# Hybrid attention/SSD layer in float32: the product of probabilities and values, the spacing of three short chains, and what is kept of the scaled tokens

## The chip, the cores and the metric

The kernel runs on one NeuronCore of one Trainium2 chip. The metric is the device time of one execution in microseconds (us). Engines are named as the profile names them: PE (TensorE matmuls), PEld (its weight loads), DVE (VectorE), ACT (ScalarE), POOL (GpSimd), SP (SyncE, which here only issues DMAs).

## The reference

One decoder layer on 2048 tokens of width 1024, everything in float32, then a final norm. Cut to its steps:

```python
mod = silu(c) @ w_ada + b_ada                    # shift1, scale1, gate1, shift2, scale2, gate2
h = modulate(rmsnorm(x, norm1_w), shift1, scale1)
q, k, v, z, xbc, dt = split(h @ w_in)            # 8 query heads, 2 key/value heads of 64
attn = sliding_window_attention(rope(q), rope(k), v, sinks)   # window 128, blocks of 128
xs, B, C = split(silu(causal_depthwise_conv(xbc)))
y = ssd_chunked_scan(xs, softplus(dt), A, B, C, d_skip)       # chunks of 128
y = group_rmsnorm(y * silu(z)) * ssm_norm_w
x = x + gate1 * (concat(attn, y) @ w_out)
h = modulate(rmsnorm(x, norm2_w), shift2, scale2)
x = x + gate2 * ((silu(h @ w_g) * (h @ w_u)) @ w_down)        # width 2816
out = rmsnorm(x, final_norm_w)
```

In the attention, for each block of 128 queries, `probs` (128 queries by 256 keys for each head) is multiplied with `v` (256 keys by 64).

## The kernel before, in words

**Tiling.** The 2048 tokens are four blocks `b` of 512 (`T`), each of four chunks of 128 (`P`). Dense projections run as pieces: one output tile in a PSUM bank (four `d` banks; four side banks `am`, `at`, `sm`, `st` belong to the mixers). Precision is kept by splitting each operand into a rounded part `hi` (type fp32r, written by ACT) and a rest `lo` (a subtraction on DVE or POOL); `mm3` (lines 280 to 282) then issues three fp32r matmuls: hi by hi, hi by lo, lo by hi.

**Order of the work.** Until the gate/up projection of the feed-forward part, PE runs in the order of the program text (`manual_schedule` of PE). There a main stream of projection pieces (`queries`, `keys_values`, `convolved`, `gated`, `out_proj`) is cut by `yield`s; after each piece `tick` lets a side stream advance by one step. Side streams are the attention (`attentions`), the SSD scan (`ssds`), the norms of later blocks, and the operands of the next stage. DVE, ACT, POOL and SP are ordered by the scheduler's own simulation when the program is built; each runs its instructions in that order, so an instruction that waits holds up all behind it on its engine. From the gate/up quads on (`quad`, lines 978 to 980), PE too is ordered by the scheduler.

**Probabilities times values.** For each chunk and each half of the heads, `transposed` (line 671) turns two tiles of probabilities on PE into the banks `am` and `at`; ACT copies each to `hi` (line 677) and DVE subtracts to get `lo` (line 678). One step later `values` (line 680) multiplies with the values. `v_ring` holds hi and lo of the values of two chunks, each padded with 64 zero columns, so that every stationary tile is 128 keys by 128 columns with one of the two key/value heads in its half and zeros in the other; `mm3` is called for each of two chunks and two heads, all four adding into one bank of 128 by 256. These are 12 fp32r matmuls of 256 columns for a half, 6 in the first chunk of all. ACT then copies the result out (line 688). `load_values` fills `v_ring` by an ACT cast (626) and a POOL subtraction (627).

**Norms.** `rstd`/`root_of_sum` give one factor for each token; `spread` (line 321) builds diagonal tiles with four DVE operations (line 324) and multiplies them by ones on PE (line 326), so that the factors stand along the free axis in a bank.

**Short chains.** `convolved` ends each piece with a chain over ACT (496, 497), DVE (498, 499), POOL (500), ACT tanh (501), DVE (502) and a store. `ssds` ends each chunk with sums of squares on ACT, an inverse root by 13 small POOL operations (250 to 255), and a scaling on ACT (805); one chunk later `turned` (line 723) transposes the result on PE (726). `out_proj` (line 819) loads its residual `x` (833, 834) after the matmuls of a piece, adds (835), and stores it to `mid` (836).

**Operands of the gate/up stage.** During the last projections (`conv`, `gated(3)`), `operands_first`, `operands_between` and `sums_ahead` read tiles of `mid`, scale them by the norm's factors (DVE, line 883), and build the operands of seven block products; `sums_ahead` leaves its four sums in DRAM (`raw_d`), from where `operands_kept` reads them when the quads begin.

Of the kernel before, what the change touches and what calls it, by code (L numbers as in the profile page):

```python
# [18 lines left out]
P = 128  # L19
# [3 lines left out]
T = 512  # L23
# [21 lines left out]
def hymba_layer(ctx, tc, xT, xtok, pos, wada, wadk, vecs, rows, wq, wkv, wz, wx, wo, wgu, wd, outT):  # L45
# [27 lines left out]
    def tmp():  # L73
        return big("t", TMP, pool=fw)
# [111 lines left out]

    def behind(engine):
        traced = nc.cur_bb.bb.instructions
        return tc.issue_after(next(i for i in reversed(traced) if i.engine == engine))
# [131 lines left out]
    def spread(y, eng=nc.vector, bc=None):  # L321
        dg, n = tmp(), y.shape[1]
        for t in range(n):
            spread.last = eng.tensor_scalar(dg[:, t * P:(t + 1) * P], ident, y[:, t:t + 1], 0.0, ALU.mult, ALU.add)
        bc = (norm_bank() if bc is None else bc)[:, 0:n * P]
        nc.tensor.matmul(bc, ones, dg[:, 0:n * P], start=True, stop=True)
        return bc
# [23 lines left out]
    def norm1(b, h):  # L351
# [9 lines left out]
        y = root_of_sum(ms, NT)  # L361
        yield
        bc = big("bc", 1, pool=xp)
        nc.scalar.copy(bc, spread(y))
# [115 lines left out]
    def convolved(b, h):  # L480
        for c in range(8):
            ps = dense()
            for half in range(2):
                if half:
                    yield
# [15 lines left out]
            nc.scalar.activation(th, cv, AF.Tanh)  # L501
            nc.vector.scalar_tensor_tensor(o, th, 1.0, cv, ALU.add, ALU.mult)
            nc.sync.dma_start(xs_d[b][c], o)
# [16 lines left out]
    v_ring = const([P, 4 * 192 + 64], "v_ring", F32R)  # L520
    nc.gpsimd.memset(v_ring.bitcast(F32), 0.0)
# [39 lines left out]
    def attentions(b, m):  # L561
        late = []

        def values_of(sms, slots, t):
            got = {}

            def turn(half):
                pT = [m.m4().rearrange("p h t -> p (h t)").rearrange("p (b j k) -> p b j k", b=4, j=2)
                      for _ in range(2)]
# [52 lines left out]
    def load_values(kv, slot):  # L622
        v = kv[:, P:2 * P].rearrange("p (r d) -> p r d", d=64)
        vhi, vlo = (v_ring[:, at:at + 256].rearrange("p (r d) -> p r d", d=P)[:, :, 0:64]
                    for at in (slot * 192, (2 + slot) * 192))
        nc.scalar.copy(vhi, v)
        nc.gpsimd.tensor_tensor(vlo, v, vhi.bitcast(F32), ALU.subtract)
# [42 lines left out]
    def transposed(sm, pT, ns, at):  # L670
# [5 lines left out]
        hi, lo = (pT[i][:, 0:2 * ns, at, :] for i in range(2))  # L676
        nc.scalar.activation(hi, ps, AF.Copy)
        nc.vector.tensor_tensor(lo, ps, hi.bitcast(F32), ALU.subtract)

    def values(out, pT, slots, half):  # L680
        po = bank("am", 1)[:, 0:2 * P]
        for s, slot in enumerate(slots):
            for r in range(2):
                b = 2 * s + r
                vhi, vlo = (v_ring[:, at:at + P] for at in (slot * 192 + r * 64, (2 + slot) * 192 + r * 64))
                phi, plo = (pT[i][:, b].rearrange("p j q -> p (j q)") for i in range(2))
                mm3(po, vhi, vlo, phi, plo, b == 0, b == 2 * len(slots) - 1)
        nc.scalar.copy(out[:, half * 2 * P:(half + 1) * 2 * P], po)

    def ssds(b, stepping, m):  # L690
# [22 lines left out]
        def decays(u, cbt):  # L713
# [7 lines left out]
            return dm  # L721

# [9 lines left out]
        for t in range(NT):  # L732
# [24 lines left out]
            u = factors(t, 1)  # L757
            yield
            if out:
                turned(*out)  # L760
                yield
# [41 lines left out]
            for g in range(2):  # L803
                gs = slice(g * 256, (g + 1) * 256)
                nc.scalar.activation(y[:, gs], y[:, gs], AF.Copy, scale=rs[:, g:g + 1])
            out = (y, o, ts)
            yield
        yield
        turned(*out)
# [12 lines left out]
    def out_proj(b, y_of, mix, bank_of, acc, norm=None, each=lambda c: None):  # L822
        for c in range(KT):
            ps = bank_of(c)
            for half in range(2):
                if half:
                    yield
# [5 lines left out]
            x = tmp()  # L833
            nc.sync.dma_start(x, xT[b, c])
# [64 lines left out]
    def operands_first(s, ops, bc):  # L899
# [4 lines left out]
        for k in range(4):  # L904
# [4 lines left out]
            if s:  # L909
                for i in range(2):  # L910
                    nc.sync.dma_start(scaled_d[i][k], h[i, 0])
# [4 lines left out]
    scaled_d = [[dr.tile([P, T], F32, name=f"scaled{i}{k}") for k in range(4)] for i in range(2)]  # L916
# [803 lines left out]
```

## Time and profile before

| | us |
|---|---|
| three timed runs of the kernel before | 2227.67, 2231.42, 2234.55 (median 2231.42) |
| the profiled execution's own time | 2235.22 |
| its span, first to last instruction | 2233.2 |
| PE busy in the span | 2167.6 (97%) |
| DVE, ACT, POOL busy | 1692.5 (76%), 1011.3 (45%), 572.5 (26%) |
| mean granted TensorE clock | 0.988 of full speed |

How to read it: a row of the groups gives line, engine, operation, output from input, shapes, count, then busy time in us and the mean ns of one, then the idle time of the engine just before these instructions and what ended it. Matmuls overlap in the pipeline, so the mean of one is longer than the distance between the starts of two that follow each other; the distance is what counts in a full queue. A float32 matmul (not fp32r) shows as two PE instructions. Names are those of the program's tiles without buffer numbers (`m` is a working tile of the mixers, `t` a tile of the ring `tmp()` of eight).

### The profile page before, as it was taken

Reading aid. Unit: us, or ns where it says so; the run is one execution under the profiler, and the core shown is the slowest. Engines: PE = TensorE matmul, PEld = TensorE weight load, DVE = VectorE, ACT = ScalarE, POOL = GpSimd, SP = SyncE. Lnnn points to the kernel's source line nnn. Section 1 sums busy time; section 2 is a strip of 40 time slices with the busy share of each in tenths; the row PEclk is TensorE's granted clock in tenths of the full one; section 3 lists DMA queues with packets and bytes.
Section 4 is the critical chain, followed back from the end, with each engine's and each line's share of the span. In section 5 each row is a group of like instructions: output and inputs, shape, how many; then the busy total and the mean of one; then the engine's idle time right before and its main releaser. Section 6 shows DMA issues by size and latency. Waiting matters only on the chain.

```text
span 2233.2 us, 33604 instructions
## 1 busy us (share of the span) xinstructions
PE 2167.6 (97%) x11108; PEld 1808.3 (81%) x11108; DVE 1692.5 (76%) x3219; ACT 1011.3 (45%) x2137; POOL 572.5 (26%) x715
## 2 busy tenths in 40 slices
PE   8979999999999899999999999999999999999998
PEld 6879897879778778888888887788888888788887
DVE  6887757777669877788887768878878875786575
ACT  3674535544444655534434535533333333544452
POOL 0213434223102311145343122242332331110011
PEclk9999999999999999999999999999999999999999
DMA  7997789786989623234333678835555535778553
GB/s 272 329 344 274 253 258 345 261 289 206 318 299 303 192 94 104 86 117 128 105 103 129 222 261 270 295 120 169 188 163 190 173 105 204 261 265 265 183 171 102
DMA packets 289181, 469.93 MB, mean 210 GB/s; under 512 B 27376, under 2 KB 97008, under 8 KB 289008
## 3 DMA queue, kind: packets, MB, share of 16 engines
q1 hardware_dynamic: 288432, 467.27, 62.9%
q8 instruction: 87, 1.43, 0.3%
q14 instruction: 86, 0.70, 0.1%
q10 hardware_dynamic: 576, 0.52, 0.1%
HBM read 334.98 MB, written 132.71 MB: 209 GB/s over the span
## 4 chain that ended last, share of the span: by engine, by line
PE 83%; DVE 7%; DMA 6%; issue 2%; ACT 2%; POOL 1%; SPq 0%; DVEq 0%; ACTq 0%; POOLq 0%
PE d L1110 16%; PE d L980 9%; PE d L978 9%; PE d L979 9%; PE d L280 5%; PE d L281 5%; PE d L282 5%; PE d L1251 1%; PE am L980 1%; PE am L978 1%; PE am L979 1%; DMA t<-in_xT_dram 1%; PE sm L791 1%; PE am L281 1%; PE am L282 1%
## 5 line engine op out<-in xcount | busy, mean ns | idle before, releaser
L1110 PE MATMUL d<-a,w 128*128 128x512 f32 x1716 | 402.9, 395 | 3.0 <-DVE w L1106 2.0
L1110 PEld LDWEIGHTS d<-a,w 128*128 128x128 f32 x1716 | 321.8, 188 | 81.1 <-DVE w L1106 2.9
L979 PE MATMUL d<-b,w 128*128 128x512 f32 x924 | 366.9, 397 | 0.9 <-DVE b L894 0.6
L978 PE MATMUL d<-b,w 128*128 128x512 f32 x924 | 365.8, 400 | 1.7 <-ACT b L893 1.3
L980 PE MATMUL d<-b,w 128*128 128x512 f32 x924 | 366.0, 397 | 0.0
L859 ACT ACTIVATE w<-s 128x512 fp32r<-128x512 f32 x176 | 110.8, 632 | 216.7 <-PE d L980 171.3
L979 PEld LDWEIGHTS d<-b,w 128*128 128x128 f32 x924 | 174.7, 189 | 41.2 <-DVE b L894 0.8
L978 PEld LDWEIGHTS d<-b,w 128*128 128x128 f32 x924 | 174.2, 189 | 40.3 <-ACT b L893 1.5
L980 PEld LDWEIGHTS d<-b,w 128*128 128x128 f32 x924 | 173.9, 188 | 39.3
L280 PE MATMUL d<-w,hl 128*128 128x256 f32 (+1 forms) x592 | 173.9, 294 | 4.8 <-DVE s L498 4.8
L281 PE MATMUL d<-w,hl 128*128 128x256 f32 (+1 forms) x592 | 169.5, 286 | 1.4 <-DVE w L273 1.4
L282 PE MATMUL d<-w,hl 128*128 128x256 f32 (+1 forms) x592 | 169.1, 286 | 0.0
L860 DVE TENSOR_TENSOR w<-s,w 128x512 fp32r<-128x512 f32 x176 | 155.4, 885 | 5.0 <-ACT w L859 4.7
L859 ACT ACTIVATE w<-raw 128x512 fp32r<-128x512 f32 x132 | 83.3, 631 | 149.3 <-PE d L980 63.0
L280 PE MATMUL d<-hl,w 128*128 128x512 f32 x352 | 146.9, 417 | 1.3 <-DMA w<-w_x 1.3
L1092 DVE TENSOR_TENSOR a<-a 128x512 fp32r<-128x512 f32 x154 | 108.5, 716 | 49.7 <-ACT a L1091 49.3
L290 POOL TENSOR_TENSOR acc<-acc,t 128x512 f32<-128x512 f32 x35 | 50.9, 1454 | 360.8 <-ACT t L289 322.6
L1106 DVE TENSOR_TENSOR w<-raw,w 128x512 fp32r<-128x512 f32 x156 | 113.3, 736 | 39.4 <-ACT w L1105 39.3
L281 PE MATMUL d<-hl,w 128*128 128x512 f32 x352 | 140.6, 399 | 1.0 <-DVE hl L819 1.0
L282 PE MATMUL d<-hl,w 128*128 128x512 f32 x352 | 140.7, 400 | 0.0
L1091 ACT ACTIVATE a<-a 128x512 fp32r<-128x512 f32 x154 | 96.1, 628 | 85.0 <-DMA a<-act_t 51.0
L1105 ACT ACTIVATE w<-raw 128x512 fp32r<-128x512 f32 x156 | 90.2, 587 | 80.1 <-PE d L1110 45.6
(426 smaller groups left out, 4943.2 us busy)
## 6 DMA issues: line engine op xcount, KB each, us to landing
raw<-in_wgu_dram SPq DMA_DIRECT2D x176, 256.0 KB, 2.9
w<-w_x SPq DMA_DIRECT2D x48, 512.0 KB, 6.2
act_t<-t SPq DMA_DIRECT2D x88, 256.0 KB, 3.1
a<-act_t SPq DMA_DIRECT2D x88, 256.0 KB, 4.4
act_b<-t SPq DMA_DIRECT2D x66, 256.0 KB, 2.0
a<-act_b SPq DMA_DIRECT2D x66, 256.0 KB, 4.2
aw<-in_wada_dram SPq DMA_DIRECT2D x64, 256.0 KB, 4.8
raw<-wd_s SPq DMA_DIRECT2D x64, 256.0 KB, 3.0
```

The source lines that it names most:

```text
L280: nc.tensor.matmul(out, ahi, bhi, start=first, stop=False)
L281: nc.tensor.matmul(out, ahi, blo, start=False, stop=False)
L282: mm3.last = nc.tensor.matmul(out, alo, bhi, start=False, stop=last)
L859: nc.scalar.activation(hi, x, AF.Copy)
L860: eng.tensor_tensor(lo, x, hi.bitcast(F32), ALU.subtract)
L978: nc.tensor.matmul(out, ahi, bhi, start=first and k == 0, stop=False, skip_group_check=True)
L979: nc.tensor.matmul(out, ahi, blo, start=False, stop=False, skip_group_check=True)
L980: mm3.last = nc.tensor.matmul(out, alo, bhi, start=False, stop=k == 3, skip_group_check=True)
L1091: nc.scalar.activation(hi, raw, AF.Copy)
L1092: nc.vector.tensor_tensor(lo, raw, hi.bitcast(F32), ALU.subtract)
L1106: nc.vector.tensor_tensor(w[1], raw, w[0].bitcast(F32), ALU.subtract)
L1110: mm3.last = nc.tensor.matmul(ps, w[x][:, ws], act[k][y], start=new and k == 0 and x + y == 0, stop=k == KP - 1 and x == 1, skip_group_che ...
```

## The change

1. `values` no longer splits. `transposed` leaves one float32 copy of the probabilities (ACT; no subtraction), `v_ring` holds the float32 values of two chunks, copied by POOL, and each product is one float32 matmul of 128 keys by 64 columns for 256 moving columns, whose output goes to partitions 0 to 63 for the first key/value head and 64 to 127 for the second, that is, through the left or right half of the array's columns.
2. `spread` is cut in two: `diagonal` (DVE) and the matmul. In `norm1` the diagonal stands one step ahead of the matmul; for `y_of[1]` it stands at piece 5 of the last projections and the matmul at piece 6.
3. The last three operations of a `convolved` piece are written half a piece later, the scaling of `ssds` two steps later (`normed`), the load of `x` in `out_proj` half a piece earlier.
4. `operands_first` stores its scaled tiles for both halves of the tokens; `operands_between` stores one more and reads one back; `sums_ahead` reads three of its four tiles back instead of scaling them again, and loads one step ahead. The three run at every piece but one. Six pieces of `convolved(3)` instead of four come before `out_proj(1)`.
5. `behind` skips the instructions of `prepared` when it looks for the one to stand behind.

The core of the diff:

```diff
     def behind(engine):
-        return tc.issue_after(next(i for i in reversed(traced) if i.engine == engine))
+        return tc.issue_after(next(i for i in reversed(traced) if i.engine == engine and i.name not in held_back))
...
-    def spread(y, eng=nc.vector, bc=None):
-        dg, n = tmp(), y.shape[1]
+    def diagonal(y):
+        n = y.shape[1]
+        dg = tmp()[:, 0:n * P]
         for t in range(n):
-            spread.last = eng.tensor_scalar(dg[:, t * P:(t + 1) * P], ident, y[:, t:t + 1], 0.0, ALU.mult, ALU.add)
-        bc = (norm_bank() if bc is None else bc)[:, 0:n * P]
-        nc.tensor.matmul(bc, ones, dg[:, 0:n * P], start=True, stop=True)
+            nc.vector.tensor_scalar(dg[:, t * P:(t + 1) * P], ident, y[:, t:t + 1], 0.0, ALU.mult, ALU.add)
+        return dg
...
     def convolved(b, h):
+        def end(c, cv, th, o):
+            nc.scalar.activation(th, cv, AF.Tanh)
+            nc.vector.scalar_tensor_tensor(o, th, 1.0, cv, ALU.add, ALU.mult)
+            nc.sync.dma_start(xs_d[b][c], o)
...
                 if half:
+                    if ending:
+                        end(*ending.pop())
                     yield
...
-    v_ring = const([P, 4 * 192 + 64], "v_ring", F32R)
-    nc.gpsimd.memset(v_ring.bitcast(F32), 0.0)
+    v_ring = const([P, 2, P], "v_ring")
...
     def load_values(kv, slot):
-        nc.scalar.copy(vhi, v)
-        nc.gpsimd.tensor_tensor(vlo, v, vhi.bitcast(F32), ALU.subtract)
+        nc.gpsimd.tensor_copy(v_ring[:, slot, :], kv[:, P:2 * P])
...
-        hi, lo = (pT[i][:, 0:2 * ns, at, :] for i in range(2))
-        nc.scalar.activation(hi, ps, AF.Copy)
-        nc.vector.tensor_tensor(lo, ps, hi.bitcast(F32), ALU.subtract)
+        nc.scalar.copy(pT[:, 0:2 * ns, at, :], ps)
...
     def values(out, pT, slots, half):
         po = bank("am", 1)[:, 0:2 * P]
         for s, slot in enumerate(slots):
             for r in range(2):
-                mm3(po, vhi, vlo, phi, plo, b == 0, b == 2 * len(slots) - 1)
+                rs = slice(r * 64, (r + 1) * 64)
+                nc.tensor.matmul(po[rs, :], v_ring[:, slot, rs], pT[:, 2 * s + r].rearrange("p j q -> p (j q)"),
+                                 start=s == 0, stop=s == len(slots) - 1)
...
             if out:
-                turned(*out)
+                normed(out[0], out[3])
+            yield
+            if out:
+                turned(*out[:3])
...
     def out_proj(b, y_of, mix, bank_of, acc, norm=None, each=lambda c: None):
                 if half:
+                    x = tmp()
+                    nc.sync.dma_start(x, xT[b, c])
                     yield
...
     def operands_between(s, ops, bc):
         for k in range(4):
-            h = scaled(s, k, bc, ((0, 0), (0, 1)))
-            nc.vector.tensor_tensor(h[0, 1], h[0, 1], h[0, 0], ALU.subtract)
-            kept(ops["t1"][k], h[0, 1])
+            (x, x00), nxt = nxt, load(k + 1) if k < 3 else None
+            with behind(mybir.EngineType.DVE):
+                h = scaled(s, k, bc, ((0, 1),), x)
+            nc.sync.dma_start(scaled_01[k], h[0, 1])
+            nc.vector.tensor_tensor(x00, h[0, 1], x00, ALU.subtract)
+            kept(ops["t1"][k], x00)
...
     def sums_ahead(s, bc):
-            h = scaled(s, k, bc, ((1, 1), (0, 1), (0, 0), (1, 0)))
+            h = fetched_mid(s, k, ((1, 1),))
+            for at, src in (((0, 1), scaled_01[k]), ((0, 0), scaled_d[s][0][k]), ((1, 0), scaled_d[s][1][k])):
+                h[at] = fetched_scaled(src)
+            yield
+            with behind(mybir.EngineType.DVE):
+                scaled(s, k, bc, ((1, 1),), h)
...
-        for _ in range(4):
+        for _ in range(6):
             take(conv, 1)
...
+            if i == 5:
+                drain(firsts)
+                dg = diagonal(y_of[1])
             if i == 6:
-                drain(firsts)
-                bcs.append(spread(y_of[1], bc=side_bank(3)))
+                bcs.append(spread(y_of[1], bc=side_bank(3), dg=dg))
```

How it moves instructions, at three places. DVE in the output projection of block 0, attention of a chunk of block 1 beside it (678 is the `lo` of the probabilities, 330 a norm's scaling, 835 the residual of `out_proj`, 658 to 664 the next probabilities). Before:

```order
L658 TENSOR_SCALAR ast<-ast 128x4
L330 SCALAR_TENSOR_TENSOR t<-t,scl_145,bc 128x512 x3
L659 TENSOR_TENSOR ast<-row,ast 128x4
L678 TENSOR_TENSOR m_6086<-am,m_6085 128x4x128
L330 SCALAR_TENSOR_TENSOR t<-t,scl_145,bc 128x512
L835 SCALAR_TENSOR_TENSOR t<-d,mod,t 128x512
L678 TENSOR_TENSOR m_6086<-at,m_6085 128x4x128
L664 TENSOR_TENSOR ast<-ast 128x4
```

After (330 is now 337, 835 is 849, 664 is 675):

```order
L761 TENSOR_TENSOR m_5986<-sm,upper 128x256
L337 SCALAR_TENSOR_TENSOR t<-t,scl_145,bc 128x512 x2
L675 TENSOR_TENSOR ast<-ast 128x4
L337 SCALAR_TENSOR_TENSOR t<-t,scl_145,bc 128x512
L676 RECIPROCAL ast<-ast 128x4
L849 SCALAR_TENSOR_TENSOR t<-d,mod,t 128x512
L715 TENSOR_TENSOR m_6368<-upper,ahi 128x512
```

Both subtractions are gone, and with them the place at which one of them stood behind the residual.

DVE beside the last projections, around the four operations of the diagonal of `y_of[1]` (324, after: 327; 260 and 262 end the inverse root, 883 and 897 scale a tile, 889 and 903 write a `lo`, 499 and 515 are of `convolved`). Before:

```order
L883 SCALAR_TENSOR_TENSOR t<-t,scl_146,sm 128x512
L260 SCALAR_TENSOR_TENSOR rstd<-rsq,rstd 128x4
L678 TENSOR_TENSOR m_8213<-at,m_8212 128x4x128
L324 TENSOR_SCALAR t<-ident,rstd 128x128 x4
L664 TENSOR_TENSOR ast<-ast 128x4
L499 SCALAR_TENSOR_TENSOR s<-cin,vec,s 128x512
```

After:

```order
L262 SCALAR_TENSOR_TENSOR rstd<-rsq,rstd 128x4
L903 SCALAR_TENSOR_TENSOR b<-t,mod,b 128x512
L327 TENSOR_SCALAR t<-ident,rstd 128x128 x4
L493 SCALAR_TENSOR_TENSOR sx<-s 128x512
L897 SCALAR_TENSOR_TENSOR t<-t,scl_146,sm 128x512 x2
L515 SCALAR_TENSOR_TENSOR s<-d,vec,s 128x512
```

Between the start of the inverse root and the diagonal there stood a half's scores (649) and two subtractions (678) before; now neither does, and the next scores (660) come behind the diagonal.

SP, two pieces of `out_proj(0)` (836, after: 850, stores `mid`; 834, after: 842, loads `x`; 271 and 276, after: 273 and 278, load and store weights). Before:

```order
L836 DMA mid_206<-t 128x512
L196 DMA aw<-in_wada_dram 128x512 x2
L585 DMA m_5736<-q_156 128x512
L834 DMA t<-in_xT_dram 128x512
L276 DMA w_o_1_5980<-w 256x1x512
L271 DMA raw<-in_wo_dram 128x512
```

After:

```order
L850 DMA mid_206<-t 128x512
L198 DMA aw<-in_wada_dram 128x512 x2
L842 DMA t<-in_xT_dram 128x512
L278 DMA w_o_1_5850<-w 256x1x512
L273 DMA raw<-in_wo_dram 128x512
L600 DMA m_5673<-q_156 128x512
```

The load of `x` stands behind the same store as before and has passed one other load.

More of the change, by code (lines that the diff above doesn't have):

```diff
@@ L567, in turn @@
             def turn(half):
[L568 to L569 removed]
+                pT = m.m4().bitcast(F32).rearrange("p h t -> p (h t)").rearrange("p (b j k) -> p b j k", b=4, j=2)
                 for j in range(2):
@@ L721, in decays, with normed @@
             return dm
+        def normed(y, rs):
+            for g in range(2):
+                gs = slice(g * 256, (g + 1) * 256)
+                nc.scalar.activation(y[:, gs], y[:, gs], AF.Copy, scale=rs[:, g:g + 1])
         def turned(y, o, ts):
@@ L802, in ssds @@
             rsqrt(rs, ss, 2, nc.gpsimd, "rss", sb)
[L803 to L806, printed above, removed]
+            out = (y, o, ts, rs)
             yield
         yield
-        turned(*out)
+        normed(out[0], out[3])
+        yield
+        turned(*out[:3])
         yield
```

47 lines of the change are left out of this document (28 added, 19 removed).

## The prediction

> **What bounds the kernel now.** I read the page first, then the table of stages, then PE's waits, then single places in the timeline.
>
> ```profile
> span 2233.2 us, 33604 instructions
> PE 2167.6 (97%) x11108; PEld 1808.3 (81%) x11108; DVE 1692.5 (76%) x3219; ACT 1011.3 (45%) x2137; POOL 572.5 (26%) x715
> ```
>
> PE is the bound, so only two things count: the length of PE's own work, and what PE waits. The stages (busy us of PE, PEld, DVE, ACT, POOL, then granted clock, DMA share, GB/s) show where it waits:
>
> ```profile
> 100.00:400.00 300.00, 282.52 (x1861) 254.54 (x1860) 209.97 (x544) 160.28 (x388) 104.80 (x186) 0.97 0.86 295
> 400.00:640.00 240.00, 226.58 (x1436) 195.56 (x1435) 171.59 (x475) 120.16 (x327) 52.55 (x106) 0.98 0.82 276
> 640.00:760.00 120.00, 108.18 (x604) 90.67 (x603) 103.06 (x213) 66.22 (x152) 32.17 (x32) 0.93 0.84 280
> 760.00:1300.00 540.00, 540.00 (x2604) 443.60 (x2603) 430.06 (x710) 240.39 (x526) 163.39 (x196) 1.00 0.39 126
> 1400.00:2233.00 833.00, 820.81 (x3683) 670.02 (x3681) 621.38 (x935) 327.79 (x570) 186.47 (x120) 1.00 0.58 190
> ```
>
> From 100 to 760 PE idles 17.5 + 13.4 + 11.8 = 42.7 us, and there alone the clock sinks visibly. From 760 to 1300 it never idles: there an edit can only change the length of PE's work. Behind 1400 the change leaves the program as it is. What ended the waits (total us, times, longest):
>
> ```profile
> PE am L281 <- DVE m L678: 7.5, 6, 3.2
> ...
> PE d L280 <- DVE s L498: 4.8, 1, 4.8
> PE st L726 <- ACT m L805: 4.5, 1, 4.5
> ...
> PE st L326 <- DVE t L324: 3.4, 1, 3.4
> ...
> PE am L280 <- DVE m L678: 1.9, 2, 1.1
> ...
> PE at L674 <- DVE m L678: 1.5, 1, 1.5
> ```
>
> The subtraction of line 678, which the change removes, ends 7.5 + 1.9 + 1.5 = 10.9 us of PE's waits. A long wait costs more than itself, since the clock falls behind it:
>
> ```profile
> 490.00:500.00 10.00, 7.41 (x29) 6.49 (x30) 6.41 (x16) 2.78 (x7) 0.34 (x1) 0.66 0.65 235
> 670.00:680.00 10.00, 7.24 (x20) 5.17 (x21) 10.00 (x24) 6.29 (x14) 1.85 (x2) 0.66 0.70 217
> ```
>
> A mean of 0.66 over 10 us is, at half speed, 6.8 us of half speed. In the first window PE idles 2.6 of them, so 4.2 us of work run at half speed: 2.1 us lost on top of the 3.2 us wait. The second gives (6.8 - 2.8) / 2 = 2.0.
>
> **Values, the length on PE.** One half of a chunk before, from the first of its 12 matmuls to the instruction behind them:
>
> ```profile
> 970.91 0.28 PE L280 MATMUL am<-m,v_ring 128*128 128x256 f32 x1
> ...
> 972.34 0.60 PE L739 MATMUL st<-ident,m 128*128 128x128 f32 x4
> ```
>
> 1.43 us, or 0.119 each. The new product is four float32 matmuls of 256 columns. The nearest row for their length is the state's product, two full-width float32 matmuls shown as four instructions, in the chain of waits:
>
> ```profile
> 262.19 0.86 PE st L779 x4
> ```
>
> That is 0.215 an instruction, two to a matmul, so eight here. Whether halves of the array overlap is seen on the scores, which use halves of its rows (64*128 is the stationary tile):
>
> ```profile
> 276.50 0.28 PE L282 MATMUL d<-w,hl 128*128 128x256 f32 x1
> 276.71 0.38 PE L640 MATMUL am<-k_ring,m 64*128 64x256 f32 x1
> 276.71 0.38 PE L640 MATMUL at<-k_ring,m 64*128 64x256 f32 x1
> ...
> 277.41 0.28 PE L640 MATMUL at<-k_ring,m 64*128 64x256 f32 x1
> 277.62 0.39 PE L280 MATMUL d<-w,hl 128*128 128x256 f32 x1
> 277.84 0.28 PE L281 MATMUL d<-w,hl 128*128 128x256 f32 x1
> ```
>
> Two matmuls on different halves start together; two on the same half follow each other. And the switch costs: from 276.50 to 277.84 there are eight places (one, six pairs, one) of 0.119, that is 0.95, but it takes 1.34, so 0.39 goes into changing over and back. No row shows halves of the columns; I take them as halves of the rows. But the two instructions of one float32 matmul use the same half, and the order is left, left, right, right: only the second of one overlaps the first of the next. Eight instructions take five places: 5 x 0.215 + 0.39 = 1.47 us against 1.43. With 30 such halves (+0.04 each) and two of the first chunk (three places and the switch, 1.04, against 0.71) this is **+2 us**. The ends: all in line, 8 x 0.215 + 0.39 = 2.11, so 30 x 0.68 + 2 x 0.54 = +21.5; overlapped and without the switch, 1.08, so 30 x -0.35 - 2 x 0.07 = -10.6. The Trainium skill, TensorEngine Tiling (Array Packing), Key Properties, says that different tiles can run weight loads and matmuls in parallel; read to the letter, by four places, the sum would be an estimated 30 x 0.21 = 6 us lower than by five.
>
> **Values, the waits.** What DVE loses:
>
> ```profile
> L678 DVE TENSOR_TENSOR m<-am,m 128x512 fp32r<-128x512 f32 x30 | 20.5, 683 | 6.4 <-ACT m L677 6.3
> L678 DVE TENSOR_TENSOR m<-at,m 128x512 fp32r<-128x512 f32 x30 | 20.4, 680 | 1.2 <-ACT m L677 1.2
> ```
>
> 41 us of DVE work, on PE's path only in the 10.9 us above. Why it was late is seen at the longest of these waits, on DVE:
>
> ```profile
> 491.19 0.75 DVE L835 SCALAR_TENSOR_TENSOR t<-d,mod,t 128x512 f32<-128x512 f32 x1 [1.75 <-DMA t<-in_xT_dram]
> 491.86 0.68 DVE L678 TENSOR_TENSOR m<-at,m 128x512 fp32r<-128x512 f32 x1
> ```
>
> The subtraction stood behind a residual that waited for its load; ACT's copy had been done long before. With the subtraction gone the copy is next. Some of it then shows, so I take 9 of 10.9, and 3 us of half speed behind the longer waits (2.1 here and about 1 for the others): **-12 us**. Bounds: -16 and -4 (if the copy is mostly as late). POOL's copy into `v_ring` waits for the previous values on PE, as ACT's cast did; behind it POOL queues the sums of `convolved` and the inverse roots, as behind the subtraction of 627 before. I cost that at nothing; if a sum comes late, `d` stays held, as at L498.
>
> **The spread.** From the inverse root's start to the end of the diagonal DVE takes 16.5 us, and has no idle time in 660 to 680:
>
> ```profile
> 656.16 0.16 DVE L303 TENSOR_SCALAR ms<-d 128x4 f32<-128x4 f32 x1 [0.74 <-PE d L295]
> 671.85 0.86 DVE L324 TENSOR_SCALAR t<-ident,rstd 128x128 f32<-128x128 f32 x4
> ```
>
> In the new order 15 full-width operations (about 0.72) and a dozen small ones (about 0.1) lie between, some 12 us; PE stopped 3.4 us before the diagonal's end, at 669.3, so it had 13 us of work from 656.2 on. The wait of 3.4 and its 2.0 of clock should go, with little to spare: **-4.5**, bounds -5.4 and 0.
>
> **The rest.** `operands_between` and `sums_ahead` lose 16 scalings:
>
> ```profile
> L883 DVE SCALAR_TENSOR_TENSOR t<-t,scl,sm 128x512 f32<-128x512 f32 x20 | 14.4, 739 | 3.1 <-DMA t<-mid 3.1
> ...
> mid<-t SPq DMA_DIRECT2D x40, 256.0 KB, 3.6
> ```
>
> 16 x 0.74 = 11.8 us of the 103 that DVE works from 640 to 760. With the other small waits on DVE I put this at -1.5. Against it stand 12 more stores of 256 KB: 3.1 MB, 11 us of DMA at that stage's 280 GB/s, where 0.16 x 120 = 19 us are free. **+3**, bounds 0 and +11. The last sums still end behind the last piece, so the quads start as before, or 1 us sooner: -1. `convolved`: in the built order the tanh stands about where it stood: -1 of the 4.8 + 1.4. `normed` later frees ACT, but POOL's inverse root, which it waits for, is as slow: -1.5 of the 4.5 + 1.9. The load of `x` stands behind the same store on SP as before, and next to the same weights: 0 (up to +2, if the ring of eight tiles runs dry and weights queue behind it). `behind`: 0.
>
> Sum: 2 - 12 - 4.5 - 1.5 + 3 - 1 - 1 - 1.5 = -16.5. The profiled execution took 2235.2, so 2218.7; it lay 3.8 above the median of the runs, 2231.4, which gives **2215 us**.
>
> **Rivals.**
>
> *The halves don't overlap.* +21.5 in place of +2: 2235, no change. For it: no row shows column halves side by side, and the two instructions of a float32 matmul may hold back the next pair. Against it: the scores' pairs. The Trainium skill, TensorE: Matmul & The Clock Gate, Part 3, says that weight loads overlap running matmuls only where the row groups differ, and that matmuls keep strict order; column halves share all row groups, so by that rule they would go in line. The full-width pair in L779 hides its loads at 0.215, so the rule is not strict here.
>
> *They overlap and the switch is nearly free,* and the waits go: 13 less, 2202. For it: a narrower weight tile; against it: 0.39 on the rows.
>
> *The waits move.* ACT's copy is as late as the subtraction was (only 4 of 12 gained) and the diagonal is no sooner (0 of 4.5): 2227.5, on the border of no change. For it: ACT's order is nearly the same, with the tanh and its wait for POOL in it. Against it: the longest wait was DVE's own queue.
>
> *Slower: tiles read back hold up SP.* A store and a load back are a chain:
>
> ```profile
> 733.39 4.30 DMA raw_t<-t
> ...
> 737.76 2.73 DMA t<-raw_t
> ```
>
> 7.0 us. Each of the four steps of `sums_ahead` reads back three such tiles; SP issues in order, so the weights of `convolved` and `gated` queue behind a load that waits for its store. It decides where the store is issued less than 7 us ahead of the load and the weights queued ahead run out: then four waits, 28 us, and about 4 of clock, 2247. Against it: the stores stand at least four pieces (over 10 us) ahead.
>
> **How the numbers follow.** A measurement tells 0.3% (6.7 us) from no change. Chances: forecast 0.45 (its own range 2206 to 2224), halves in line 0.17, free switch 0.12, waits move 0.15, SP held up 0.11. Faster by over 0.3%, below 2224.7: nearly all of the first, all of the third, half of the fourth, a sixth of the second: 0.66. Slower, above 2238.1: most of the last and a quarter of the second: 0.14. The rest, 0.20, is no change. The range reaches from the free switch with 9 us of spread (2193) to the halves in line with 3 more (2238).
>
> **What would show it.** In the profile after: the distance from the first of L694's instructions to the next of PE (1.47; 2.1 in line; 1.1 free); no wait of PE on a subtraction at L694, under 2 us on ACT's copy; no wait for the spread at `st`; DVE from 640 to 760 some 20 us shorter; PE's idle time from 100 to 760 down from 42.7 to about 27. The prediction is wrong if that idle time does not fall, if it falls and PE's busy time rises by as much, or if SP waits for stores in front of weights.

## The result, and the profile after

| | us |
|---|---|
| the changed kernel, four timed runs | 2208.76, 2211.43, 2213.70, 2217.11 (median 2212.56) |
| the kernel before, four runs | 2227.67 to 2234.70 (median 2232.99) |
| ratio | 0.9913, 95% interval 0.9887 to 0.9940 |
| the same kernels timed once more (six and 17 runs) | ratio 0.9912, interval 0.9893 to 0.9931 |
| profiled execution of the changed kernel | 2211.43, span 2209.7 |

So the change makes the kernel faster by 0.9%, some 20 us; 2215 us (range 2193 to 2238) was forecast. The total is close. The runs below show that this is luck: errors in its terms cancel.

The page of the changed kernel, first lines:

```profile
span 2209.7 us, 33269 instructions
...
PE 2152.7 (97%) x10984; PEld 1773.3 (80%) x10984; DVE 1645.7 (74%) x3139; ACT 1010.5 (46%) x2121; POOL 572.0 (26%) x714
```

Its stages (busy us of PE, PEld, DVE, ACT, POOL, clock, DMA share, GB/s), to be held against those of before:

```profile
100.00:400.00 300.00, 288.33 (x1890) 255.40 (x1890) 204.82 (x525) 159.14 (x381) 106.59 (x185) 0.97 0.88 299
400.00:640.00 240.00, 226.50 (x1396) 188.30 (x1395) 166.43 (x468) 121.80 (x330) 54.00 (x108) 0.99 0.88 294
640.00:760.00 120.00, 111.43 (x644) 88.21 (x643) 93.51 (x222) 76.92 (x185) 32.42 (x31) 0.97 0.81 277
760.00:1300.00 540.00, 539.13 (x2549) 436.92 (x2548) 416.08 (x672) 233.82 (x497) 161.70 (x197) 1.00 0.41 133
```

PE idles 11.7 + 13.5 + 8.6 = 33.8 us from 100 to 760; it was 42.7, and 27 was forecast. The clock rose from 0.93 to 0.97 from 640 to 760 and hardly changed before. Windows of fixed time hold other pieces in a kernel that runs ahead, so here is one stretch of the program, from the matmul of the spread that starts at 382.0 before (380.1 after) to the ones-matmul of `rstd` in the first `out_proj`, at 549.8 (534.1). Before:

```profile
382.00:549.80 167.80, 154.97 (x998) 135.87 (x997) 123.65 (x308) 88.85 (x238) 47.53 (x89) 0.95 0.77 259
```

After:

```profile
380.10:534.10 154.00, 146.19 (x970) 125.09 (x969) 119.40 (x295) 83.35 (x221) 48.50 (x82) 1.00 0.83 276
```

This stretch is 13.8 us shorter: 5.0 less idle time, and a clock of 1.00 in place of 0.95; five halves of `values` in it give 1.1 by their length (below). Not all of this is owed to the values. In the trace before, the stretch has 17.1 us at half speed, from 388.7, 416.0 and 491.1 on; the trace after has none. Two of the three:

```profile
388.70:395.50 6.80, 5.22 (x15) 4.14 (x16) 3.50 (x7) 4.40 (x10) 1.84 (x6) 0.50 0.49 164
491.10:497.90 6.80, 5.31 (x18) 4.73 (x19) 4.89 (x13) 2.59 (x6) 0.00 (x0) 0.50 0.73 261
```

Only that from 491.1 lies at a wait for the subtraction. That from 388.7 lies at the wait of 4.5 us for the scaled tokens of `ssds`, that from 416.0 behind waits of 1.0 and 1.4 us for the keys and queries (L640). After, the first of these waits is 0.5 us and the other two are not there. The next stretch, up to the first matmul of the quads (724.3 before, 700.2 after), is 8.4 shorter; the quads 0.8. What ended PE's waits after:

```profile
PE d L282 <- DVE s L515: 6.6, 2, 4.8
PE sm L333 <- DVE t L327: 5.6, 2, 3.7
...
PE am L694 <- ACT m L687: 4.0, 4, 1.4
...
PE st L739 <- ACT m L734: 0.5, 1, 0.5
```

The subtraction is gone from the list, and the copy (L687) shows with 4.0 us instead; the scaled tokens (`normed`, now L734) fell from 4.5 to 0.5; the spread no longer waits at `st`. But another spread, that of `y_of[0]` at `sm`, now waits 3.7 (1.0 before; the other of 1.9 is near the end of the program, before and after). The convolution (now L515) keeps its wait of 4.8 and has got one of 1.8 beside it.

The new product, one half in the timeline of PE:

```profile
228.97 0.39 PE L284 MATMUL d<-hl,w 128*128 128x512 f32 x1
229.28 1.08 PE L694 MATMUL am<-m,v_ring 128*64 128x256 f32 x8
230.30 0.50 PE L282 MATMUL d<-hl,w 128*128 128x512 f32 x1
230.64 0.40 PE L283 MATMUL d<-hl,w 128*128 128x512 f32 x1
```

Eight instructions take 1.02 us from the first start to the next instruction. In the trace they start in four pairs, the two of a pair 6 to 7 ns apart, the second pair 0.267 after the first and the next two 0.216 after the one before. The gaps around them are 0.31 and 0.34 where matmuls of 512 columns stand 0.23 apart.

### The profile page after: what moved, and what is told of

It is laid out like the page before. It is cut to its first block, busy times and chain, and to the rows that moved or that the text cites. A ratio compares the mean times of both kernels' runs of the same rounds, so it can differ in the third digit from the quotient of the medians.

```text
span 2209.7 us, 33269 instructions
## 1 busy us (share of the span) xinstructions
PE 2152.7 (97%) x10984; PEld 1773.3 (80%) x10984; DVE 1645.7 (74%) x3139; ACT 1010.5 (46%) x2121; POOL 572.0 (26%) x714
## 4 chain that ended last, share of the span: by engine, by line
PE 79%; DMA 7%; DVE 6%; issue 3%; ACT 2%; POOL 2%; SPq 1%; DVEq 0%; POOLq 0%; ACTq 0%
PE d L1141 16%; PE d L1009 9%; PE d L1011 9%; PE d L1010 9%; PE d L282 5%; PE d L283 5%; PE d L284 5%; PE d L1282 1%; PE am L1011 1%; PE am L1009 1%; PE am L1010 1%; DMA a<-act_t 1%; PE sm L1011 1%; PE sm L1009 1%; PE sm L1010 1%
## 5 line engine op out<-in xcount | busy, mean ns | idle before, releaser
L1123 DVE TENSOR_TENSOR a<-a 128x512 fp32r<-128x512 f32 x154 | 107.8, 712 | 47.5 <-ACT a L1122 47.2
```

The costliest lines, as they stand in the source:

```text
L1123: nc.vector.tensor_tensor(lo, raw, hi.bitcast(F32), ALU.subtract)
```

## The experiments

The stretches in the table run from matmul to matmul of the same kind in each trace, in us: A up to 382.0 of before (from the spread at 108.5), B from there to `rstd` of the first `out_proj` (549.8), C to the first quad matmul (724.3), D the quads up to the first matmul of the down projection (1348.7). "Half speed" is the time in A, B, C and D for which the trace records a granted clock of 0.50 (all other records of these 14 traces say 1.00; nearly all stays at 0.50 last 3.4 us or a whole multiple of it). "Idle" is PE's idle time from the start of A to the end of D. The ratio is to the kernel before, timed beside it.

Two profiles of the changed kernel differ by 0.6 to 1.5 in a stretch, but the noise is larger than that. In stretch A, DVE, ACT and POOL run the same instructions in the same order, and PE has the same program, in the changed kernel, its repetition and experiments 5, 8, 9 and 10 (a few records are missing in each); yet A takes 268.3 to 274.9, with 10.2 to 20.5 us of it at half speed. So a difference of up to some 6 us in one stretch of one profile can be chance, and the stretches only say where to look; the ratios rest on four to twelve runs.

| kernel | ratio (95% interval) | A | B | C | D | half speed in A, B, C, D | idle |
|---|---|---|---|---|---|---|---|
| before | | 273.5 | 167.8 | 174.5 | 624.4 | 10.2, 17.1, 10.2, 6.8 | 42.7 |
| changed | 0.9913 (0.9887 to 0.9940) | 274.0 | 154.0 | 166.1 | 623.6 | 17.1, 0, 6.8, 6.8 | 34.6 |
| 11 changed again | 0.9912 (0.9893 to 0.9931) | 274.6 | 155.5 | 166.9 | 624.5 | 20.5, 3.4, 6.8, 10.2 | 34.8 |
| 1 values only | 0.9906 (0.9889 to 0.9923) | 274.0 | 157.6 | 164.3 | 622.7 | 20.5, 10.2, 3.4, 10.2 | 32.2 |
| 2 values back | 1.0018 (1.0007 to 1.0030) | 275.8 | 160.2 | 179.0 | 626.5 | 20.5, 6.8, 13.8, 6.6 | 42.4 |
| 3 by half | 0.9920 (0.9904 to 0.9936) | 274.6 | 156.3 | 168.8 | 621.6 | 20.5, 3.4, 10.2, 0 | 36.8 |
| 4 full width | 0.9983 (0.9973 to 0.9994) | 275.5 | 162.5 | 170.1 | 629.0 | 10.2, 13.7, 3.4, 3.4 | 35.9 |
| 5 operands back | 0.9889 (0.9869 to 0.9908) | 272.1 | 153.6 | 169.6 | 618.6 | 10.2, 0, 6.8, 3.4 | 35.8 |
| 6 x back | 0.9919 (0.9899 to 0.9938) | 271.2 | 155.5 | 170.0 | 621.8 | 10.2, 3.4, 10.2, 0 | 37.4 |
| 7 chains back | 0.9939 (0.9920 to 0.9957) | 269.2 | 156.2 | 161.5 | 628.2 | 6.8, 6.8, 3.4, 10.2 | 33.4 |
| 8 diagonal early | 0.9878 (0.9857 to 0.9898) | 274.9 | 154.2 | 158.1 | 623.2 | 20.5, 0, 0, 0 | 33.0 |
| 9 combined | 0.9892 (0.9873 to 0.9910) | 268.3 | 153.0 | 168.4 | 616.9 | 10.2, 0, 10.2, 6.8 | 28.7 |
| 10 four pieces | 0.9900 (0.9883 to 0.9917) | 271.2 | 154.7 | 171.1 | 620.0 | 10.2, 3.4, 10.2, 0 | 39.3 |
| 12 idle subtraction | 0.9967 (0.9953 to 0.9980) | 271.8 | 153.6 | 172.6 | 627.5 | 10.2, 0, 10.2, 10.2 | 41.5 |

My theory was that the product of probabilities and values brings the gain, by fewer waits and (as seen after) by its length. The rival was that the other edits, the earlier load of `x` above all, cured the waits.

**1. Values only.** The kernel before with part 1 of the change alone:

```diff
-    v_ring = const([P, 4 * 192 + 64], "v_ring", F32R)
+    v_ring = const([P, 2, P], "v_ring")
...
-        nc.vector.tensor_tensor(lo, ps, hi.bitcast(F32), ALU.subtract)
+        nc.scalar.copy(pT[:, 0:2 * ns, at, :], ps)
...
-                mm3(po, vhi, vlo, phi, plo, b == 0, b == 2 * len(slots) - 1)
+                nc.tensor.matmul(po[rs, :], v_ring[:, slot, rs], ...)
```

> The kernel before with the float32 values alone (no split, column halves, one copy by ACT, POOL copies the values). Theory 1, the values bring most of the change: a half takes 1.20 us on PE in place of 1.43 (30 halves, -7), and the waits on the subtraction (10.9 us, about 3 more at half speed behind them) give way to waits on ACT's copy of about 4, so -9: some 16 us in all, about 2217. Theory 2, the residual that waited for its load is what made the subtraction late, and the earlier load in the output projection cured it: then here the waits only move to ACT's copy or to what stands behind the residual, only the length is gained and some 2 us of wait, about 2224.

Measured: 2210.26 us, ratio 0.9906, 21 us less. Part 1 alone gives the whole gain. Its waits (here 326 is the spread's matmul, 796 the scaling of `ssds`, 677 and 670 are product and copy):

```profile
PE d L280 <- DVE s L498: 4.8, 1, 4.8
...
PE st L717 <- ACT m L796: 4.3, 2, 3.0
...
PE sm L326 <- DVE t L324: 3.2, 2, 1.9
PE st L326 <- DVE t L324: 2.3, 1, 2.3
...
PE am L677 <- ACT m L670: 0.8, 1, 0.8
```

The load of `x` stands where it stood, and the wait of 3.2 us at 493 (with its half speed, the largest single place in the prediction's -12) is gone all the same: at that place this trace gains 5.3 us on the one before, the 3.2 + 2.1 of the prediction. The copy is hardly waited for. PE's idle time falls by 10.5 us, about what the subtraction's waits were.

**2. Values back.** The changed kernel with part 1 undone, so the rest of the change alone.

> The changed kernel with only the values as before (split in two parts, twelve matmuls a half, subtraction on DVE). The spread at st, the normed and the operands keep their edits. Theory 1: the values' 16 us are lost, 2212.6 + 16 = about 2229, and PE waits for the subtraction again for about 8 to 11 us. Theory 2: the earlier load of x has taken away the longest of those waits, so only the length and a few us are lost: about 2221.

Measured: 2236.07, ratio 1.0018, 4 us slower than before. The rest gains nothing; it costs. Where:

```profile
PE st L333 <- DVE t L327: 7.1, 1, 7.1
...
PE am L283 <- DVE m L695: 2.1, 6, 0.8
```

The waits for the subtraction have indeed shrunk, from 10.9 to 2.4 (stretch B is 7.6 shorter), so theory 2 was right about these waits; which part of the edit did it is not shown. But PE's idle time is 42.4 us, as before: the waits have moved. The spread at `st`, which the diagonal one piece ahead was to relieve, waits 7.1 in place of 3.4. Neither theory had that.

**3. By half.** Left, left, right, right instead of left, right, left, right:

```diff
-        for s, slot in enumerate(slots):
-            for r in range(2):
+        for r in range(2):
+            for s, slot in enumerate(slots):
```

> The changed kernel with the two loops of the values exchanged: left, left, right, right in place of left, right, left, right; the same eight instructions. Theory A, a matmul on one half of the columns starts beside one on the other half only where the two are neighbours in the queue: now only one pair of neighbours differs, so about 7 places of 0.216 and 0.34 for the switch, 1.85 us a half in place of 1.20; 30 x 0.65 = +20, about 2232. Theory B, each half of the array has a queue of its own and the order does not matter: 1.20 us as before, the same time. Theory C, a part of it: the queue looks a few instructions ahead, 1.4 to 1.6 us, +6 to +12.

Measured: ratio 0.9920, the same time, and the same length:

```profile
295.68 0.28 PE L284 MATMUL d<-w,hl 128*128 128x256 f32 x1
295.89 1.09 PE L694 MATMUL am<-m,v_ring 128*64 128x256 f32 x8
296.91 0.39 PE L282 MATMUL d<-w,hl 128*128 128x256 f32 x1
297.13 0.28 PE L283 MATMUL d<-w,hl 128*128 128x256 f32 x1
```

Theory B holds: the order does not matter, each half goes through its four instructions on its own. These neighbours have 256 columns, so the switch is read cleanly: 0.09 ahead (0.21 - 0.12), 1.02 - 4 x 0.216 = 0.16 within, 0.10 behind (0.22 - 0.12), 0.35 in all.

**4. Full width.** Each head of the values padded to 128 columns, four float32 matmuls into one output:

```diff
+    v_ring = const([P, 2 * 192], "v_ring")
+    nc.gpsimd.memset(v_ring, 0.0)
...
+                nc.tensor.matmul(po, v_ring[:, at:at + P], pT[:, b].rearrange("p j q -> p (j q)"),
+                                 start=b == 0, stop=b == 2 * len(slots) - 1)
```

> The changed kernel with the float32 values at full width: each value head is padded with 64 zero columns, four float32 matmuls of 128 by 128 a half, all into one output; no halves of the array, so no switch. POOL copies the values in two parts. 8 x 0.216 = 1.73 us a half in place of 1.20. Theory 1, PE's length is paid one for one: 30 x 0.53 = +16, about 2229, and the waits stay those of the changed kernel. Rival, part of the length falls where PE waits for other engines anyway: only about +8, 2221.

Measured: ratio 0.9983, 0.0070 or 15.6 us above the changed kernel. One half:

```profile
292.96 0.28 PE L284 MATMUL d<-w,hl 128*128 128x256 f32 x1
293.08 1.89 PE L697 MATMUL am<-m,v_ring 128*128 128x256 f32 x8
294.62 0.47 PE L282 MATMUL d<-w,hl 128*128 128x256 f32 x1
294.93 0.28 PE L283 MATMUL d<-w,hl 128*128 128x256 f32 x1
```

No gap ahead, and 1.54 + 0.31 - 0.12 = 1.73 us, eight places. That is 0.52 more than 0.09 + 1.02 + 0.10 = 1.21 with halves; 30 x 0.52 = 15.6. The difference of the two ratios is known to some 6 us either way, so length is paid one for one within that, and the theory that only half of it is paid (8 us) is just excluded. One stretch bears it out: with the same 10.2 us at half speed in A, experiment 4 takes 275.5 and experiments 5, 6, 10 and 12 take 271.2 to 272.1 (and 9 takes 268.3); six halves make 3.1. By this the length in the changed kernel is worth an estimated 30 x (1.43 - 1.21), about 6.6 us.

**5. Operands back.** The changed kernel with part 4 undone (the old `operands_first`, `operands_between`, `sums_ahead`, their steps, four pieces of `convolved(3)`).

> The changed kernel with the operands of the gate/up stage as before (no tiles stored and read back, four pieces of the convolution ahead of the output projection, the old steps); the diagonal for the second spread still stands one piece ahead of its matmul. Theory 1, as in the prediction: the scalings saved and the stores added nearly cancel, so within 2 us of the changed kernel. Theory 2, the operands' edit costs what the rest of the change costs beside the old values (5 us): then about 2207. Theory 3, it brings the quads forward: undone, about 2216.

Measured: ratio 0.9889, 5 us below the changed kernel; the intervals overlap. By the stretches the gain is in the quads (5.0 to 5.9, of which half speed, 3.4 us here against 6.8 and 10.2, makes an estimated 2 to 3), while the spread at `st` loses more than the one at `sm` gains:

```profile
PE st L333 <- DVE t L327: 6.9, 1, 6.9
...
PE sm L333 <- DVE t L327: 2.8, 2, 1.9
```

**6. x back.** The changed kernel, the load of `x` behind the piece again:

```diff
                 if half:
-                    x = tmp()
-                    nc.sync.dma_start(x, xT[b, c])
                     yield
...
+            x = tmp()
+            nc.sync.dma_start(x, xT[b, c])
             nc.vector.scalar_tensor_tensor(x, ps, gate1[:, c:c + 1], x, ALU.mult, ALU.add)
```

> The changed kernel with the load of x in the output projection where it was, behind the piece's matmuls. Theory 1: nothing, within 2 us, since without the subtraction nothing that PE needs at once stands behind the residual on DVE. Theory 2: the earlier load also keeps the residual, the diagonal and the keys early: undone, the wait for the spread at sm (3.7) and others grow, 3 to 6 us more, about 2217. Theory 3: the earlier load holds a tile of the ring for half a piece and delays others: undone, the wait at sm falls to the 1.9 that the kernel with the values alone has, 2 to 4 us less.

Measured: ratio 0.9919. No effect of the edit can be told from none.

**7. Chains back.** The changed kernel with the ends of `convolved` and the `normed` where they were.

> The changed kernel with the ends of convolved and the scaling of ssds (normed) where they were. Theory 1, a trade: the wait of PE for normed comes back (0.5 to about 4.3, as in the kernel with the values alone), while the waits for ACT's copy of the probabilities (4.0) go to under 1, as there: within 2 us of the changed kernel. Theory 2, as in the prediction, the spacing gives 2.5 us: 2215.

Measured: ratio 0.9939, 6 us above the changed kernel; the intervals overlap from 0.9920 to 0.9931. Waits of PE (725 is the scaling here, 678 the copy):

```profile
PE st L730 <- ACT m L725: 4.0, 2, 2.7
...
PE am L685 <- ACT m L678: 1.8, 2, 1.0
```

`st` waits for the scaling again, the copy's waits fall from 4.0 to 1.8: the trade of theory 1. The profiles differ by only 1.4 us in span, and this profile is of the fastest of its six runs, so whether the spacing gains 6 us or nothing stays open; a gain of the size forecast (2.5) fits both.

**8. Diagonal early.** PE's longest new wait is that at `sm`. DVE around it in the changed kernel (849 is the residual of the last piece, 613 and 620 make the keys and the queries):

```profile
624.30 0.69 DVE L292 TENSOR_TENSOR acc<-acc,t 128x512 f32<-128x512 f32 x1 [0.70 <-ACT t L291]
631.32 0.75 DVE L849 SCALAR_TENSOR_TENSOR t<-d,mod,t 128x512 f32<-128x512 f32 x1 [6.33 <-DMA t<-in_xT_dram]
631.99 0.28 DVE L613 TENSOR_TENSOR k_ring<-am,k_ring 128x128 fp32r<-128x128 f32 x1
632.18 0.86 DVE L327 TENSOR_SCALAR t<-ident,rstd 128x128 f32<-128x128 f32 x4
```

DVE stands 6.3 us behind a residual whose `x` has not landed, and the diagonal, whose factors were ready long before, stands behind that. So it is written one piece earlier:

```diff
-        run(out_proj(1, y_of, mix, lambda c: dense(), sums()), 0.5)
+        dgs = []
+        run(out_proj(1, y_of, mix, lambda c: dense(), sums(),
+                     each=lambda c: dgs.append(diagonal(y_of[0])) if c == KT - 2 else None), 0.5)
...
+        bcs, ops = [spread(y_of[0], bc=side_bank(2), dg=dgs[0])], {}
```

> The changed kernel with the diagonal of the first block's norm written after the last piece but one of the second output projection, so that DVE builds it ahead of the residual that waits for its load; the matmul stays. Theory 1: the wait of 3.7 us at sm goes, with about 1.5 us of half speed behind it: 5 us less, about 2207.5. Theory 2: the keys that stand behind the same residual are next (the scores a piece later wait for them): 1 to 2 us less, 2211.

Measured: 2204.70, ratio 0.9878, the lowest of all. The wait is gone (the one at `sm` that is left is another, near the end of the program), and the clock of that stage is full:

```profile
PE sm L333 <- DVE t L327: 1.9, 1, 1.9
```

```profile
640.00:760.00 120.00, 111.28 (x651) 87.89 (x650) 100.85 (x226) 80.31 (x196) 33.54 (x31) 1.00 0.83 286
```

Stretch C falls from 166.1 to 158.1, an estimated 3 us of it because the half speed in this stretch (6.8 us in both profiles of the changed kernel) is gone too. Against the two timings of the changed kernel this is 0.34% or 8 us less; taking the two intervals as independent, the difference is 0.0034 with some 0.0028 to either side. It is faster than both kernels.

**9. Combined.** Experiment 5 with the early diagonal of 8, and the matmul of the second spread at piece 7 instead of 6.

> The changed kernel with the operands as before, the first diagonal early (both as in the two runs before), and the matmul of the second spread one piece later, its four steps of operands_between behind it likewise. Theory 1, the gains add: the operands' 5 us stay, and the wait of 6.9 us at st in the kernel with the operands as before goes with about 3 us of half speed: some 2200. Theory 2, the wait moves on to the operands that now start a piece later (a wait at the first quads): 2207, as with the operands alone.

Measured: ratio 0.9892, as with the operands alone (0.9889). The gains don't add. The later matmul still waits:

```profile
PE at L616 <- DMA m<-q: 6.4, 2, 3.5
PE st L333 <- DVE t L327: 5.8, 1, 5.8
```

From the root's first operation (L305, at 633.10) to the diagonal's end (654.33) DVE takes 21.2 us here: the scheduler has spread the root's small steps over the added time.

**10. Four pieces.** The changed kernel with `range(4)` in place of `range(6)` alone.

> The changed kernel with only the six pieces of the convolution ahead of the second output projection put back to four; the tiles stored and read back stay. Theory 1, the six pieces cost the 5 us that the operands' edit costs in all (the spread at sm waits 3.7 there, about 1 with four): then the time falls by about 4 beside the changed kernel. Theory 2, the stores and the read-back cost it: no difference.

Measured: ratio 0.9900, 2.7 us below the changed kernel, which the intervals don't tell from it. The long wait at `sm` goes with the six pieces, as theory 1 had it (1.2 us there in place of 3.7), but the wait at `st` is 6.9 again, and stretch C is 4 to 5 us longer. The quads are 3.6 to 4.5 shorter, much as in experiment 5; but this profile has no half speed in them, and against the others without any (experiments 3, 6 and 8, 621.6 to 623.2) they are 1.6 to 3.2 shorter. So the six pieces seem to trade one for the other, and no cost of the stores and the read-back is seen. Whether the quads are longer behind six pieces, and why, is open.

**11. The changed kernel again.**

> The changed kernel itself, so that the others of this call stand beside it on one chip and its own time is known better: 2213, ratio 0.9915.

Measured: ratio 0.9912, as expected.

**12. Idle subtraction.** The changed kernel with DVE's 41 us put back, without anyone who waits for the result:

```diff
+                spare = m.m4().rearrange("p h t -> p (h t)").rearrange("p (b j k) -> p b j k", b=4, j=2)
...
+                    x = pT[:, 0:2 * len(slots), j, :]
+                    nc.vector.tensor_tensor(spare[:, 0:2 * len(slots), j, :], x, x, ALU.subtract)
```

> The changed kernel with a subtraction put back on DVE for each half's two tiles, as long as those of line 678 were and behind the same copies, but read from the copy and written to a tile that nothing reads: DVE does the 41 us again, PE and the banks do not wait for it. Theory 1, the waits went because PE no longer depends on the subtraction: within 2 us of the changed kernel. Theory 2, they went because DVE has 41 us less in its queue, so that everything else on it is sooner: 6 us or more are lost, about 2219.

Measured: ratio 0.9967, 12 us above the changed kernel (its profiled execution, at the low end of its runs, has a span 2 to 7 above theirs). Its groups show the added work, 47.5 us, somewhat more than the 41 removed:

```profile
L589 DVE TENSOR_TENSOR m<-m 128x512 fp32r<-128x512 f32 (+1 forms) x64 | 47.5, 762 | 9.2 <-ACT m L690 8.9
```

And PE's waits show what it delays:

```profile
PE st L333 <- DVE t L327: 7.0, 1, 7.0
...
PE am L697 <- ACT m L690: 4.9, 4, 2.7
```

Stretch B stays at 153.6: there the put-back time costs nothing. C goes back from 166.1 to 172.6 by the spread at `st`: there the gain came from DVE's time. D is longer by 3 to 4, near the noise. Idle time rises from 34.6 to 41.5. The added work also holds one more tile of the mixers' ring, as before, which this run does not separate from DVE's time.

Experiments 2, 12 and the changed kernel are three steps of one stair, all with the rest of the change. The values together bring 23 us there (1.0018 to 0.9913). From 2 to 12 (1.0018 to 0.9967, 11 us) it is mainly the length and the dependence that change, which leaves about 5 for the dependence; from 12 to the changed kernel (12 us) the put-back work goes. These differences are known to 4 to 6 us either way.

## Why the prediction was right in the sum, and where it was wrong

**Values, the length (+2): wrong.** The step that failed is "the order is left, left, right, right: only the second of one overlaps the first of the next. Eight instructions take five places". They take four, in whatever order they are written (experiment 3), and the switch costs 0.35 rather than 0.39. A half falls from 1.43 to 1.21 us, so the term is about -6.6. What the Trainium skill's TensorEngine Tiling (Array Packing), Key Properties, says by the letter, loads and matmuls of different tiles in parallel, agrees with the trace. The rule of the Trainium skill's TensorE: Matmul & The Clock Gate, Part 3, on row groups and strict order, which was named beside the rival of 2235, does not: the column halves share all rows, and their loads are recorded 6 ns apart and their matmuls 7 (from 293.48 on in the changed kernel).

**Values, the waits (-12): about right in size, with one cause too few.** Part 1 alone gives 21 us (17 to 25 by the interval); less the length that is about -14 (-11 to -18), so -12 can't be told from it. The longest wait went as worked out (5.3 us with its half speed). But the waits are not the whole of it: in experiment 2 they were nearly gone with the old values, and the time was no better. And "41 us of DVE work, on PE's path only in the 10.9 us above" is not so: put back without any dependence, this work costs some 12 us, and the chains on DVE that then come later are seen, the root and diagonal of the second spread above all (the tile that it holds is not separated). The copy took the place of the subtraction with 4.0 us in the changed kernel, twice the bound of 2 set for it; in the kernel with the values alone it was 0.8.

**The spread (-4.5): wrong in its reason.** The wait at `st` did go, and the root with its diagonal took 12.5 us (647.83 to 660.33) against the 12 counted; the first of its operations and the last on DVE, after:

```profile
647.83 0.15 DVE L305 TENSOR_SCALAR ms<-d 128x4 f32<-128x4 f32 x1
...
659.45 0.88 DVE L327 TENSOR_SCALAR t<-ident,rstd 128x128 f32<-128x128 f32 x4
```

But the early place of the diagonal isn't what shortened it: with it, yet with the subtractions (experiment 2) or with DVE's time put back (12), or with four pieces (5 and 10), the same chain takes 19.5 to 20.0 and PE waits about 7, more than the 3.4 of before (16.5 for the chain); in experiment 2:

```profile
660.74 0.16 DVE L305 TENSOR_SCALAR ms<-d 128x4 f32<-128x4 f32 x1
...
679.90 0.86 DVE L327 TENSOR_SCALAR t<-ident,rstd 128x128 f32<-128x128 f32 x4
```

With the values alone it takes 15.4 and PE waits 2.3. PE waits less than 1.2 us only where the new values and the six pieces come together (experiments 3, 4, 6, 7 and 8 too) and nothing is put back on DVE. And the wait of `y_of[0]` at `sm` grew to 3.7, which the prediction did not look at: a residual behind a load.

**Operands (-1.5, +3, -1), chains (-1, -1.5), x (0).** The x edit is nothing, as said. Of the rest no term is resolved by itself; together with the spread they were put at -6.5 and come out at +4 (1.6 to 6.7) beside the old values and, from 0.9906 against 0.9912, at nothing that can be told beside the new ones. DVE from 640 to 760 did fall, by 9.5 us instead of 20 (with other pieces in the window).

So the length was 9 us better than forecast, the waits about 2 (within their error), and the rest some 7 to 10 worse; the sum hid this, and its closeness is luck. Of the rivals, the halves in line are refuted by the 1.21 us, and so is the free switch, since the switch costs 0.35; its -10.6 for the length was still nearer to -6.6 than the +2. The waits did move in part (4.0 to the copy, 3.7 to `sm`), but less than they shrank. SP was held up by read-backs as that rival had it, behind four loads of stored tiles, but for 7.6 us in all in place of 28, and PE waited for no weight there (its one wait for a weight, 2.1 us, is at 205):

```profile
SPq L934 <- DMA scaled<-t: 7.6, 4, 3.7
```

## What to carry to other kernels

Taking work off an engine that is only 76% busy can be worth as much as removing the waits that name it (here some 12 us against about 5 for the dependence, both roughly known): the engine's other chains move up. Putting the time back without the dependence shows it. And a wait that goes is not yet a gain: in experiment 2 the named waits fell by 8.5 us and PE's idle time stayed. Where an engine's order is made by a scheduler, an operation written earlier is not run earlier as a matter of course; look at what stands ahead of it, above all at something that waits for a load. And a total that comes out near the forecast is no evidence for its terms: one run with a part alone and one with all but that part told more than the total. Before a stretch of one profile is compared with that of another, look at the half speed in both.

## What the runs showed of the hardware

Two float32 products on the left and right 64 columns of the array ran side by side: four pairs of instructions, 6 to 7 ns apart in the changed kernel and 13 to 14 ns in the other order, 0.216 us a pair for 256 columns (the first 0.267), the same as one full-width instruction (experiment 4). The change to halves and back cost 0.34 to 0.35 us for a group, and the order of left and right within the group made no difference.

The granted clock was 1.00 or 0.50 in every record. Stays at 0.50 followed waits of PE far shorter than themselves: 3.4 us from 416.0 before, behind waits of 1.0 and 1.4 us. A matmul of 512 columns, 0.23 us after the one before elsewhere, came 0.43 after it in such a stay (635.40 and 635.83 in the changed kernel).
